# The convolution branch's output projection as seven products of quarters, with weight sums made by adding transfers

## The chip, the cores and the metric

The kernel runs on one core of a Trainium2 chip. The metric is the device time of one execution in microseconds (us). Three runs of the kernel before took 323.69, 324.17 and 324.25 us; their median is 324.17 us. The engines are named as in the profile: PE is TensorE's matrix multiplication and PEld its weight loads, DVE is VectorE, ACT is ScalarE, POOL is GpSimd, SP is SyncE. A q behind a name (SPq, POOLq) is the engine's sequencer, which issues transfers.

## The reference

One decoder layer on a sequence of 256 positions of width 1024, all in float32. What matters here, cut to its core:

```
h = rmsnorm(x, norm_g) * (1 + scale) + shift
q, k, v, g_attn, cb, cc, cx, g_conv, m_attn, m_conv = split(h @ w_in)
attn   = moba_attention(q, k, v, rel_bias)
y_attn = (attn * silu(g_attn)) @ w_o_attn
y_conv = (short_conv(cb, cc, cx, conv_w) * silu(g_conv)) @ w_o_conv
merged = sigmoid(m_attn) * y_attn + sigmoid(m_conv) * y_conv
out    = rmsnorm(x + gate * (merged @ w_out), final_g)
```

Every matrix here is 1024 wide, so `y_conv` is a product of a 256x1024 matrix with a 1024x1024 matrix. With both cut in four quarters, the rows of the left one at 128 and every other side at 512, it takes eight products of quarters and four additions in the usual way.

## The kernel before

Every float32 product is made of three passes. Each operand is split into a high part, rounded to the matrix unit's fast float32 format, and the rest, its low part; the product is high by high, high by low and low by high. For a weight tile (128x2048, 1 MB, one transfer on SP's queue, `load`, L58) ACT makes the high part and DVE the low part (`split`, L63: tiles named `...h` and `...l`). The raw tiles rotate through five buffers (L50), the high and the low parts through three each (L46), so a split waits until PE has finished with the tile three places back, and a load until the tile five places back is split.

The work that the change touches lies in the last third. `rows_half` (L362) computes two 128x512 results, one for each half t of the positions, from two weight tiles kh: `rows_mm` (L352) issues 12 matmuls for each t and tile, so a tile is 24 matmuls. In the order of the program: the merge gates `ma` and `mc` (L502 to L506, with ACT's sigmoid into SA and SC), then `merged(0)` and `merged(1)` (L537), each one column half n: `oa`, the attention branch's projection, then `oc`, the convolution branch's, from GA and GC, and the merging on DVE into MR (L541, L547, L548). `turned(n)` (L528) transposes MR on PE (tiles `pm`) and splits it into M, the left operand of the last projection `wo`, whose results are `ao`. `turned(0)` stands ahead of `oc` of the second half, `turned(1)` inside the first product `ao`.

A scheduler orders each engine's instructions by when it thinks that they can start, except those marked `pin`. Each engine runs its own list in order and waits on semaphores. PSUM's eight banks are handed out in turn (L52).

At the program's start `warm(WARM2)` (L254) puts matmuls on a tile of ones, whose results nobody reads, between the transposes of the first and of the second half of the normalised input (`px`, L205). ACT's first `hf` (L257) needs the transposes behind them, and PE's first real products need `hf`.

Of the kernel before, what the change touches and what calls it, by code (L numbers as in the profile page):

```python
# [39 lines left out]
def layer_kernel(ctx: ExitStack, tc, x, c, vec, wp_all, slab_all, onehot, final_g, out):  # L40
    nc = tc.nc
    x, out = x[0], out[0]

# [458 lines left out]
    for blk, dst in (("ma", SA), ("mc", SC)):  # L502
        for n in range(2):
            m = rows_half(blk, n, H)
            for t in range(2):
                nc.scalar.activation(dst[:, t, 512 * n:512 * (n + 1)], m[t], AF.Sigmoid)  # L506
# [30 lines left out]
    def merged(n):  # L537
        cols = slice(512 * n, 512 * (n + 1))
        ya = rows_half("oa", n, GA)
        for t in range(2):  # L540
            nc.vector.tensor_mul(MR[:, t, cols], ya[t], SA[:, t, cols])  # L541
        if n:
            turned(0)
        yc = rows_half("oc", n, GC)
        for t in range(2):
            p = tp.tile([P, 512], F32, tag="cx", name=f"yc{n}{t}", bufs=2)
            nc.vector.tensor_mul(p, yc[t], SC[:, t, cols])  # L547
            nc.vector.tensor_add(MR[:, t, cols], MR[:, t, cols], p)  # L548

    merged(0)  # L550
    merged(1)
# [145 lines left out]
```

## Time and profile before

| | |
|---|---|
| median of three runs | 324.17 us |
| the profiled execution | 324.17 us, of which 322.4 us are the span of the trace |
| outside the span | 1.77 us |
| PE busy | 312.5 us (97%) |
| DVE, ACT, POOL busy | 236.8, 176.2, 7.4 us |
| granted TensorE clock, mean | 0.994 of full speed |

The span runs from the first to the last instruction. Busy is not the same as bound: PE is the engine whose next instruction nearly always stands ready.

### The profile page before, as it was taken

The numbers are of one execution on the slowest core, as the hardware profiler recorded it, in microseconds if no ns is written. First come the engines' busy times: TensorE is split into PE (matmuls) and PEld (weight loads), VectorE is DVE, ScalarE is ACT, GpSimd is POOL, SyncE is SP. The second block draws the span as 40 slices with busy tenths as digits, with TensorE's granted clock in tenths as the row PEclk, the third lists the DMA queues.
The fourth block names the chain that finished last, engine by engine and source line by source line (L and its number), as shares of the span: only waits on it lengthen the run. The fifth ranks groups of instructions, "written<-read, shape, count | busy, mean of one in ns | idle before, by whom it ended". The sixth has DMA issues, their size and how long they took to land.

```text
span 322.4 us, 4585 instructions
## 1 busy us (share of the span) xinstructions
PE 312.5 (97%) x1794; PEld 275.3 (85%) x1794; DVE 236.8 (73%) x355; ACT 176.2 (55%) x271; POOL 7.4 (2%) x17
## 2 busy tenths in 40 slices
PE   7899999999999999999999999999999999999992
PEld 6799999888888988889888888888888888888892
DVE  3899994968599999786977787865243457657774
ACT  2655565863676777476666657474444433351430
POOL 2400000000000000000000000000000000000010
PEclk9999999999999999999999999999999999999997
DMA  7999999986676385836344577446465756300003
GB/s 271 413 411 409 407 415 416 399 330 259 246 266 236 138 355 184 287 126 256 130 138 188 197 254 269 138 151 233 159 232 164 285 162 239 132 0 0 0 2 130
DMA packets 14187, 72.74 MB, mean 226 GB/s; under 512 B 1510, under 2 KB 2902, under 8 KB 8022
## 3 DMA queue, kind: packets, MB, share of 16 engines
q1 hardware_dynamic: 12528, 70.40, 58.1%
q10 hardware_dynamic: 1606, 2.05, 1.8%
q8 instruction: 14, 0.23, 0.3%
q14 instruction: 7, 0.06, 0.0%
q0 software_dynamic: 32, 0.01, 0.0%
HBM read 71.39 MB, written 1.06 MB: 225 GB/s over the span
## 4 chain that ended last, share of the span: by engine, by line
PE 93%; DMA 2%; issue 1%; DVE 1%; ACT 1%; SPq 0%; POOL 0%; POOLq 0%; DVEq 0%; ACTq 0%
PE acc L198 15%; PE agc L340 5%; PE aga L340 5%; PE acc L340 5%; PE acx L340 5%; PE acb L340 5%; PE aga L342 2%; PE agc L342 2%; PE acb L342 2%; PE acx L342 2%; PE acc L342 2%; PE aoa L355 2%; PE ama L355 2%; PE av L355 2%; PE av L356 2%; PE aoc L356 2%
## 5 line engine op out<-in xcount | busy, mean ns | idle before, releaser
L381 DVE CUSTOM_DVE_ANT_0 gate<-gate,csb,vT 128x1024 f32<-128x1024 f32 x8 | 10.1, 1276 | 0.0
L161 DVE CUSTOM_DVE_ANT_0 ada<-ada,csb,msc 128x1024 f32<-128x1024 f32 x7 | 9.4, 1341 | 0.0
L161 DVE CUSTOM_DVE_ANT_0 ada<-ada,csb,vT 128x1024 f32<-128x1024 f32 x7 | 8.9, 1278 | 0.0
L589 POOL TENSOR_TENSOR rf<-ms,mhalf 128x1 f32<-128x1 f32 x2 | 1.7, 828 | 302.4 <-DVE ms L616 298.8
L326 ACT ACTIVATE lowcb<-acb 128x256 f32<-128x256 f32 x8 | 3.0, 371 | 6.1 <-PE acb L342 6.1
L347 ACT ACTIVATE M<-pm 128x512 fp32r<-128x512 f32 x4 | 2.2, 590 | 6.7 <-PE pm L534 6.7
L571 ACT ACTIVATE SQ<-TT 128x512 f32<-128x512 f32 x3 | 1.9, 628 | 7.1 <-DVE TT L566 7.1
L506 ACT ACTIVATE SC<-amc 128x512 f32<-128x512 f32 x4 | 2.4, 599 | 5.8 <-PE amc L357 5.8
L506 ACT ACTIVATE SA<-ama 128x512 f32<-128x512 f32 x4 | 2.4, 600 | 5.3 <-PE ama L357 5.3
L139 PE MATMUL wt<-ones 128*128 128x128 f32 x22 | 4.2, 362 | 1.0 <-DVE ones L127 1.0
L396 DVE TENSOR_TENSOR AX<-QK,AX 128x128 fp32r<-128x128 f32 (+1 forms) x16 | 5.1, 348 | 0.0
L70 DVE TENSOR_TENSOR oc00l<-woc,oc00h 128x2048 fp32r<-128x2048 f32 x1 | 2.3, 2292 | 3.8 <-ACT oc00h L69 3.8
L374 ACT ACTIVATE V<-av 128x512 f32<-128x512 f32 x4 | 2.4, 599 | 4.8 <-PE av L357 4.8
L70 DVE TENSOR_TENSOR oa00l<-woa,oa00h 128x2048 fp32r<-128x2048 f32 x1 | 2.3, 2291 | 3.6 <-ACT oa00h L69 3.6
L70 DVE TENSOR_TENSOR cb0l<-wcb,cb0h 128x2048 fp32r<-128x2048 f32 x1 | 2.3, 2293 | 3.6 <-ACT cb0h L69 3.6
L70 DVE TENSOR_TENSOR mc10l<-wmc,mc10h 128x2048 fp32r<-128x2048 f32 x1 | 2.3, 2291 | 3.6 <-ACT mc10h L69 3.6
L395 ACT ACTIVATE AX<-QK 128x128 fp32r<-128x128 f32 (+1 forms) x16 | 4.8, 364 | 0.0
L326 ACT ACTIVATE lowga<-aga 128x256 f32<-128x256 f32 x8 | 3.0, 373 | 3.3 <-PE aga L342 3.3
L139 PEld LDWEIGHTS wt<-ones 128*128 128x128 f32 x22 | 3.8, 267 | 1.0 <-DVE ones L127 1.0
L469 ACT ACTIVATE y<-cc,vT 128x256 f32<-128x256 f32 x8 | 3.9, 500 | 1.4 <-DVE cc L465 1.4
L326 ACT ACTIVATE lowgc<-agc 128x256 f32<-128x256 f32 x8 | 3.0, 373 | 3.0 <-PE agc L342 3.0
L70 DVE TENSOR_TENSOR oa11l<-woa,oa11h 128x2048 fp32r<-128x2048 f32 x1 | 2.3, 2293 | 3.1 <-ACT oa11h L69 3.1
(497 smaller groups left out, 1102.0 us busy)
## 6 DMA issues: line engine op xcount, KB each, us to landing
ada<-in_wp_dram SPq DMA_DIRECT2D x16, 512.0 KB, 10.2
slab<-in_slab_dram SPq DMA_DIRECT2D x16, 512.0 KB, 10.2
wv<-in_wp_dram SPq DMA_DIRECT2D x4, 1024.0 KB, 11.3
wcc<-in_wp_dram SPq DMA_DIRECT2D x4, 1024.0 KB, 5.6
wcx<-in_wp_dram SPq DMA_DIRECT2D x4, 1024.0 KB, 4.9
gate<-in_wp_dram SPq DMA_DIRECT2D x4, 1024.0 KB, 6.5
wcb<-in_wp_dram SPq DMA_DIRECT2D x4, 1024.0 KB, 5.4
wgc<-in_wp_dram SPq DMA_DIRECT2D x4, 1024.0 KB, 4.9
```

The costliest lines, as they stand in the source:

```text
L70: pin(nc.vector.tensor_sub(lo[:, s], raw[:, s], hi[:, s].bitcast(F32)))
L139: pin(nc.tensor.matmul(wt[:, 0:P], ones, ones, start=True, stop=True))
L161: pin(nc.vector.tensor_tensor_reduce(src, src, csb, vT[:, i:i + 1] if s else 1.0, bias(i, s), ALU.mult, ALU.add, scs[:, i, s:s + 1]))
L198: pin(nc.tensor.matmul(acc[j // 2][:, (j % 2) * S:(j % 2 + 1) * S], w[i][:, j * P:(j + 1) * P], x, start=(i == 0 and j // 2 not in opened) ...
L326: nc.scalar.activation(low, a[:, S:], AF.Copy)
L340: nc.tensor.matmul(a, hi[:, k, cols], rhs[:, k, :], start=(k == 0), stop=False)
L342: nc.tensor.matmul(a[:, S:], lo[:, k, cols], rhs[:, k, 0:S], start=False, stop=(k == KT - 1))
L355: nc.tensor.matmul(a, xh, hi[:, k4, cols], start=(first and k4 == 0), stop=False)
L356: nc.tensor.matmul(a, xh, lo[:, k4, cols], start=False, stop=False)
L381: nc.vector.tensor_tensor_reduce(src, src, csb, 1.0, vT[:, 24 + d:25 + d], ALU.mult, ALU.add, gcol[:, d:d + 1])
L395: nc.scalar.activation(hi, src, AF.Copy)
L396: nc.vector.tensor_sub(lo, src, hi.bitcast(F32))
```

## The change

`y_conv` is computed by Strassen's scheme in Winograd's form. With the four left quarters F(t, kh) and the four weight quarters, each of them one tile `oc` n kh, it takes seven products p1 to p7 instead of eight, each of 12 matmuls and one weight tile. Three of them (p1, p2, p3) use a weight quarter as it is, four use sums of two, three or four quarters:

- p7: oc10 + oc11, in the tile T2
- p5: oc10 + oc00, in the raw tile wt1
- p6: T2 + oc00, added onto the same tile once p7 has split it
- p4: T2 + oc01, added once p6 has split it

The sums are made by transfers on POOL's queue that add what they bring to what lies in the tile (`add_on`). The four left sums v1 to v4 are made on DVE from F, which is GC's high and low parts added together, and split into SX. Three PSUM banks hold the partial results for the whole stretch, and the ring of the others shrinks to five for it.

The products are woven between the tiles of `mc` and `oa`; on PE the order is now ma, p7, mc00, p5, mc01, p1, mc10, p6, mc11, p2, oa00, p4, oa01, p3, oa10, `turned(0)`, oa11, and then `ao`. The transposition of the gate column (`pgt`), from which gb is read back, moves behind p4. The merging on DVE is now in SA (`joined`). T2, and after it gb and fg, take the place of csb, cs, gb and fg in one 8 KB tile. The x tile XR is loaded later. And WARM2 falls from 5 to 3. The diff's core:

```diff
-WARM2 = 5
+WARM2 = 3
...
+    ring, turn = list(range(8)), [0]
+
+    def bank(name, at=None):
+        if at is None:
+            at = ring[turn[0] % len(ring)]
+            turn[0] += 1
+        return ps.tile([P, 512], F32, tag=f"b{at}", name=name)
...
+    F = raw_tile([P, 2048], "F").rearrange("p (k n) -> p k n", k=KT)
+    nc.vector.tensor_add(F, GC[:, :, 0:S].bitcast(F32), GC[:, :, S:].bitcast(F32))
...
+    def both(v, dst):
+        nc.scalar.activation(dst[:, :, 0:P], v, AF.Copy)
+        nc.vector.tensor_sub(dst[:, :, P:], v, dst[:, :, 0:P].bitcast(F32))
...
+    T2 = big.tile([P, 2048], F32, tag="W2", name="T2")
+    def add_on(t, key):
+        nc.gpsimd.dma_start(t, wp_all[UNIT[key]], accum_op=ALU.add)
+
+    nc.sync.dma_start(T2, wp_all[UNIT["oc", 1, 0]])
+    add_on(T2, ("oc", 1, 1))
+    first = load(("oc", 1, 0), "wt1")
+    add_on(first, ("oc", 0, 0))
+    ring[:] = range(3, 8)
+    turn[0] = 0
+    bA, bB, bC = [bank(f"str{i}", i) for i in range(3)]
+
+    def product(a, raw, name, first, s=0, t=0, kh=0):
+        hi, lo = split(raw.rearrange("p (k n) -> p k n", k=4), [P, 4, 512], name)
...
+    product(bB, T2, "p7", True, s=3)
+    q7 = kept(bB, "cx", "q7")
+    add_on(T2, ("oc", 0, 0))
+    a = pair("mc", 0)
+    rows_tile("mc", 0, 0, H, a)
+    product(bC, first, "p5", True, s=1)
+    rows_tile("mc", 0, 1, H, a)
...
+    product(bB, T2, "p6", False, s=2)
+    u3 = tp.tile([P, 512], F32, tag="cc", name="u3", bufs=2)
+    nc.vector.tensor_add(u3, bB, q1)
+    nc.vector.tensor_sub(q7, u3, q7)
+    nc.vector.tensor_sub(u3, bC, u3)
+    rows_tile("mc", 1, 1, H, a)
...
+    product(bA, w21, "p2", False, t=0, kh=1)
+    add_on(T2, ("oc", 0, 1))
+    nc.vector.tensor_mul(part(0, 0), part(0, 0), bA)
+    a = pair("oa", 0)
+    rows_tile("oa", 0, 0, GA, a)
+    product(bB, T2, "p4", False, t=1, kh=1)
...
+    joined(0, a)
+    product(bC, load(("oc", 1, 1), "woc22"), "p3", False, s=4)
...
+    turned(0)
+    rows_tile("oa", 1, 1, GA, a)
+    joined(1, a)
+    ring[:] = range(8)
```

Three places show how the lists of the engines move. On ACT, where the high parts of the weight tiles are made in the stretch of the gates, the list before has one tile `...h` after another:

```order
L69 ACTIVATE mc00h<-wmc_2317 128x2048 [waits DMAHW0_49,Activation_49]
L69 ACTIVATE mc01h<-wmc_2347 128x2048 [waits DMAHW1_49,PE_49,Activation_49]
L506 ACTIVATE SA<-ama_2251 128x512 [waits PE_49]
L506 ACTIVATE SA<-ama_2252 128x512 [waits PE_49]
L69 ACTIVATE mc10h<-wmc_2381 128x2048 [waits DMAHW2_49,DVE_49]
L69 ACTIVATE mc11h<-wmc_2411 128x2048 [waits DMAHW3_49,DVE_49,PE_49]
```

The same engine now, from the second half of the gate mc to p4 (DMAHW are transfers of SP's and ACT's queues, DMASW those of POOL's):

```order
L514 ACTIVATE SC<-amc_2359 128x512 [waits PE_49]
L74 ACTIVATE p6h<-T_2330 128x2048 [waits DMASW3_49,DVE_49]
L579 ACTIVATE q_2456<-str_2336 128x512 [waits PE_49]
L74 ACTIVATE mc11h<-wmc_2510 128x2048 [waits DMAHW4_49,DVE_49]
L74 ACTIVATE p2h<-woc_2543 128x2048 [waits DMAHW5_49,DVE_49,PE_49]
L74 ACTIVATE oa00h<-woa_2565 128x2048 [waits DMAHW6_49,DVE_49,PE_49]
L514 ACTIVATE SC<-amc_2458 128x512 [waits PE_49]
L514 ACTIVATE SC<-amc_2459 128x512 [waits PE_49]
L74 ACTIVATE p4h<-T_2330 128x2048 [waits DMASW4_49,DVE_49]
L74 ACTIVATE oa01h<-woa_2621 128x2048 [waits DMAHW0_49,DVE_49,PE_49]
```

The product tiles stand between the tiles of the gates and of `oa`, and p6h and p4h wait for a transfer of POOL's queue; what follows them in ACT's list stands behind that wait.

On POOL the list of the changed kernel, from the start's last work to the end, is this (before, nothing stood between `rvd` and `rf`):

```order
L278 DMA rvd<-rv 8x384 [waits Activation_49]
L555 DMA T_2330<-in_wp_dram 128x2048 [waits DMAHW4_49,DVE_49,PE_49]
L555 DMA wt_2333<-in_wp_dram 128x2048 [waits DMAHW3_49,DMAHW5_49,DMAHW2_49,DMAHW6_49,DMAHW0_49,DMAHW7_49,DVE_49,Activation_49]
L555 DMA T_2330<-in_wp_dram 128x2048 [waits DMASW1_49,DVE_49]
L555 DMA T_2330<-in_wp_dram 128x2048 [waits DMASW3_49,DVE_49]
L703 TENSOR_TENSOR rf_2892<-ms_2890,mhalf 128x1 [waits DVE_49,Pool_49]
```

The third and the fourth adding transfer each wait for the one before on the same tile and for DVE's low part of the product that used the tile's older contents.

On DVE, ahead of the last projection, the list before ran so (`M<-pm` is the low part of the transposed merged rows, `yc` and `MR` the merging of the second half):

```order
L541 TENSOR_TENSOR MR<-aoa_2586,SA 128x512
L70 TENSOR_TENSOR o00l<-wo_2731,o00h 128x2048
L348 TENSOR_TENSOR M<-pm_2649,M 128x2x256
L348 TENSOR_TENSOR M<-pm_2656,M 128x2x256
L70 TENSOR_TENSOR o01l<-wo_2737,o01h 128x2048
L547 TENSOR_TENSOR yc_2725<-aoc_2663,SC 128x512
```

and now so:

```order
L75 TENSOR_TENSOR o00l<-wo_2756,o00h 128x2048
L636 TENSOR_TENSOR SC<-SC,q_2355 128x512
L647 TENSOR_TENSOR wo_2809<-wo_2809,gf 128x4x256
L75 TENSOR_TENSOR o01l<-wo_2762,o01h 128x2048
L353 TENSOR_TENSOR M<-pm_2708,M 128x2x256
L353 TENSOR_TENSOR M<-pm_2715,M 128x2x256
L629 TENSOR_TENSOR SA<-SA,aoa_2675 128x512
L631 TENSOR_TENSOR SA<-SA,SC 128x512
```

The low parts of M come behind both splits of `wo`'s first tiles, and the merging of the second half follows them at once.

## Rows read from the trace of the kernel before

**Rows 1.** The page: span, busy time of the first engines, chain that ended last.
```profile
span 322.4 us, 4585 instructions
PE 312.5 (97%) x1794; PEld 275.3 (85%) x1794; DVE 236.8 (73%) x355; ACT 176.2 (55%) x271; POOL 7.4 (2%) x17
...
PE 93%; DMA 2%; issue 1%; DVE 1%; ACT 1%; SPq 0%; POOL 0%; POOLq 0%; DVEq 0%; ACTq 0%
```

**Rows 2.** Waits of PE, whole span: engine, tile, releaser: us, times, longest.
```profile
PE px L205 <- DVE xx L243: 2.0, 1, 2.0
PE wt L139 <- DVE ones L127: 1.0, 1, 1.0
PE acc L198 <- ACT hf L257: 0.7, 1, 0.7
```

**Rows 3.** Timeline, PE, 281 to 293: start us, us, engine, line, operation, tiles.
```profile
281.31 1.03 PE L534 MATMUL pm<-ident,MR 128*128 128x128 f32 x8
...
282.64 0.39 PE L357 MATMUL aoc<-oc10h,GC 128*128 128x512 f32 x1
...
293.07 0.39 PE L355 MATMUL ao<-o00h,M 128*128 128x512 f32 x1
```

**Rows 4.** Timeline, ACT and DVE, one weight tile's split.
```profile
270.62 1.92 ACT L69 ACTIVATE oc10h<-woc 128x2048 fp32r<-128x2048 f32 x1 [3.52 <-PE aoc L357]
...
272.57 2.29 DVE L70 TENSOR_TENSOR oc10l<-woc,oc10h 128x2048 fp32r<-128x2048 f32 x1 [0.50 <-ACT oc10h L69]
```

**Rows 5.** Windows: stretch, length, busy PE, PEld, DVE, ACT, POOL, clock, DMA, GB/s.
```profile
205.00:227.00 22.00, 22.00 (x100) 18.20 (x99) 13.40 (x12) 11.12 (x13) 0.00 (x0) 1.00 0.53 187
227.00:249.00 22.00, 22.00 (x99) 18.16 (x98) 9.17 (x4) 10.08 (x9) 0.00 (x0) 1.00 0.56 194
249.00:271.00 22.00, 22.00 (x99) 18.18 (x98) 12.01 (x9) 8.39 (x7) 0.00 (x0) 1.00 0.59 214
271.00:293.00 22.00, 22.00 (x103) 18.31 (x102) 14.63 (x13) 8.26 (x6) 0.00 (x0) 1.00 0.24 92
```

**Rows 6.** A group of DVE instructions on 128x512: count | busy us, mean ns | idle.
```profile
L548 DVE TENSOR_TENSOR MR<-MR,yc 128x512 f32<-128x512 f32 x4 | 2.8, 692 | 0.1
```

**Rows 7.** DMA issues, whole span: count, KB each, median us to landing.
```profile
woc<-in_wp_dram SPq DMA_DIRECT2D x4, 1024.0 KB, 4.9
...
BI<-rvd ACTq DMA_DIRECT2D x1, 1024.0 KB, 18.5
...
rvd<-rv POOLq DMA_DIRECT2D x1, 12.0 KB, 5.3
```

**Rows 8.** Timeline, DVE, ACT, POOL, 281 to 297, around the last projection.
```profile
281.50 1.92 ACT L69 ACTIVATE o00h<-wo 128x2048 fp32r<-128x2048 f32 x1 [3.53 <-PE aoa L357]
283.32 1.07 ACT L347 ACTIVATE M<-pm 128x512 fp32r<-128x512 f32 x2
...
285.66 1.28 DVE L348 TENSOR_TENSOR M<-pm,M 128x512 fp32r<-128x512 f32 x2
```

**Rows 9.** Timeline, all engines, 7 to 13, the start.
```profile
9.83 1.28 PE L139 MATMUL wt<-ones 128*128 128x128 f32 x10
...
9.94 0.51 ACT L240 ACTIVATE xx<-xx,r 128x256 f32<-128x256 f32 x1 [0.95 <-POOL r L145]
10.01 2.22 POOL L241 TENSOR_SCALAR xx<-xx,r 128x768 f32<-128x768 f32 x1
10.66 0.08 DVE L154 DVE_READ_ACCUMULATOR2_ANT scs<- 128x1 f32 x1
...
10.95 0.38 PE L205 MATMUL px<-ident,xx 128*128 128x128 f32 x2
11.37 0.56 ACT L257 ACTIVATE hf<-px,scs 128x256 f32<-128x256 f32 x1 [0.92 <-DVE csb L220]
...
12.95 0.82 PE L205 MATMUL px<-ident,xx 128*128 128x128 f32 x6
```

**Rows 10.** Timeline, PE, first matmuls of the span.
```profile
1.05 2.93 PE L139 MATMUL wt<-ones 128*128 128x128 f32 x12 [1.05 <-DVE ones L127]
```

More of the change, by code (lines that the diff above doesn't have):

```diff
@@ L50, in layer_kernel @@
     RAW_BUFS = 5
-    def bank(name):
-        return ps.tile([P, 512], F32, tag="acc", name=name, bufs=8)
+    ring, turn = list(range(8)), [0]
[4 more added lines that the diff above has]
+        return ps.tile([P, 512], F32, tag=f"b{at}", name=name)
     def raw_tile(shape, name):
@@ L79, in layer_kernel @@
     xnT = big.tile([P, KT, S], F32, tag="BI", name="xnT")
-    csb = big.tile([P, D], F32, tag="AG", name="csb")
-    cs = big.tile([P, P], F32, tag="GB", name="cs")
+    wide = big.tile([P, 2 * D], F32, tag="W2", name="wide")
+    csb, cs = wide[:, 0:D], wide[:, D:D + P]
     crows = const.tile([KT, P], F32, name="crows")
@@ L497, in layer_kernel, with rows_tile @@
         gated("ga", AT, GA, j)
-    gb = big.tile([P, D], F32, tag="GB", name="gb")
-    XR = big.tile([P, 2, D], F32, tag="YB", name="XR")
     SA = big.tile([P, 2, D], F32, tag="V", name="SA")
     SC = big.tile([P, 2, D], F32, tag="BI", name="SC")
[L502 to L506, printed above, removed]
+    def rows_tile(blk, n, kh, xs, a):
+        raw = load((blk, n, kh), f"w{blk}{n}{kh}").rearrange("p (k n) -> p k n", k=4)
+        hi, lo = split(raw, [P, 4, 512], f"{blk}{n}{kh}")
+        for t in range(2):
+            rows_mm(a[t], xs, t, hi, lo, 4 * kh, slice(0, 512), kh == 0, kh == 1)
@@ new lines, in gate_rows, with pair @@
+    def gate_rows(blk, n, dst, a):
+        for t in range(2):
+            nc.scalar.activation(dst[:, t, 512 * n:512 * (n + 1)], a[t], AF.Sigmoid)
+    def pair(blk, n):
+        return [bank(f"a{blk}{n}{t}") for t in range(2)]
+    for n in range(2):
+        a = pair("ma", n)
+        for kh in range(2):
+            rows_tile("ma", n, kh, H, a)
+        gate_rows("ma", n, SA, a)
+    F = raw_tile([P, 2048], "F").rearrange("p (k n) -> p k n", k=KT)
+    nc.vector.tensor_add(F, GC[:, :, 0:S].bitcast(F32), GC[:, :, S:].bitcast(F32))
@@ new lines, in layer_kernel, with quarter, quad @@
+    SX = [big.tile([P, 2, 4, S], F32R, tag=tag, name=f"SX{tag}") for tag in ("YB", "AT")]
+    SX = {1: SX[0][:, 0], 3: SX[0][:, 1], 2: SX[1][:, 0], 4: SX[1][:, 1]}
+    def quarter(t, kh):
+        return F[:, 4 * kh:4 * kh + 4, t * P:(t + 1) * P]
+    def quad(tag, name):
+        return tp.tile([P, 4, P], F32, tag=tag, name=name, bufs=2)
+    def both(v, dst):
+        nc.scalar.activation(dst[:, :, 0:P], v, AF.Copy)
+        nc.vector.tensor_sub(dst[:, :, P:], v, dst[:, :, 0:P].bitcast(F32))
@@ new lines, in layer_kernel @@
+    v3 = quad("cc", "v3")
+    nc.vector.tensor_sub(v3, quarter(0, 0), quarter(1, 0))
+    both(v3, SX[3])
+    v1 = quad("cx", "v1")
+    nc.vector.tensor_sub(v1, quarter(1, 0), quarter(1, 1))
+    both(v1, SX[1])
+    v2 = quad("y", "v2")
+    nc.vector.tensor_sub(v2, v1, quarter(0, 0))
+    both(v2, SX[2])
+    v4 = quad("cc", "v4")
+    nc.vector.tensor_add(v4, v2, quarter(0, 1))
+    both(v4, SX[4])
+    T2 = big.tile([P, 2048], F32, tag="W2", name="T2")
+    def add_on(t, key):
+        nc.gpsimd.dma_start(t, wp_all[UNIT[key]], accum_op=ALU.add)
@@ new lines, in layer_kernel @@
+    nc.sync.dma_start(T2, wp_all[UNIT["oc", 1, 0]])
[7 more added lines that the diff above has]
+        hi, lo = split(raw.rearrange("p (k n) -> p k n", k=4), [P, 4, 512], name)
+        for k in range(4):
+            if s:
+                xh, xl = SX[s][:, k, 0:P], SX[s][:, k, P:]
+            else:
+                xh = GC[:, 4 * kh + k, t * P:(t + 1) * P]
+                xl = GC[:, 4 * kh + k, S + t * P:S + (t + 1) * P]
+            for w, xp, end in ((hi, xh, False), (lo, xh, False), (hi, xl, k == 3)):
+                nc.tensor.matmul(a, xp, w[:, k], start=(first and k == 0 and w is hi and xp is xh), stop=end,
+                                 skip_group_check=True)
@@ new lines, in kept, with part @@
+    def kept(a, tag, name):
+        t = tp.tile([P, 512], F32, tag=tag, name=name, bufs=2)
+        nc.scalar.activation(t, a, AF.Copy)
+        return t
+    def part(t, n):
+        return SC[:, t, 512 * n:512 * (n + 1)]
+    product(bB, T2, "p7", True, s=3)
[5 more added lines that the diff above has]
+    rows_tile("mc", 0, 1, H, a)
+    gate_rows("mc", 0, SC, a)
+    w11 = load(("oc", 0, 0), "woc11")
@@ new lines, in layer_kernel @@
+    product(bA, w11, "p1", True, t=0, kh=0)
+    q1 = kept(bA, "y", "q1")
+    a = pair("mc", 1)
+    rows_tile("mc", 1, 0, H, a)
+    product(bB, T2, "p6", False, s=2)
[4 more added lines that the diff above has]
+    rows_tile("mc", 1, 1, H, a)
+    gate_rows("mc", 1, SC, a)
+    nc.vector.tensor_mul(part(1, 1), part(1, 1), u3)
+    w21 = load(("oc", 0, 1), "woc21")
@@ L507, in layer_kernel @@
+    product(bA, w21, "p2", False, t=0, kh=1)
[4 more added lines that the diff above has]
+    product(bB, T2, "p4", False, t=1, kh=1)
+    nc.vector.tensor_add(q1, bB, q1)
+    nc.vector.tensor_mul(part(1, 0), part(1, 0), q1)
+    gf = big.tile([P, 2 * D], F32, tag="W2", name="gf")
+    gb, fg = gf[:, 0:D], gf[:, D:]
     pgt = bank("pgt")
@@ L513, in layer_kernel, with joined @@
     nc.scalar.dma_start(gb, bass.AP(tensor=gd.tensor, offset=gd.offset, ap=[[0, P], [1, D]]))
-    nc.sync.dma_start(XR, x.rearrange("(t p) d -> p t d", p=P))
+    rows_tile("oa", 0, 1, GA, a)
+    def joined(n, a):
+        cols = slice(512 * n, 512 * (n + 1))
+        for t in range(2):
+            nc.vector.tensor_mul(SA[:, t, cols], SA[:, t, cols], a[t])
+        for t in range(2):
+            nc.vector.tensor_add(SA[:, t, cols], SA[:, t, cols], SC[:, t, cols])
+    joined(0, a)
+    product(bC, load(("oc", 1, 1), "woc22"), "p3", False, s=4)
+    nc.vector.tensor_sub(q7, bC, q7)
+    nc.vector.tensor_mul(part(0, 1), part(0, 1), q7)
+    a = pair("oa", 1)
+    rows_tile("oa", 1, 0, GA, a)
     M = big.tile([P, KT, 512], F32R, tag="H", name="M")
@@ L524, in wo_split @@
         wo[n, kh] = split(raw, [P, 4, 512], f"o{n}{kh}", 1, pin)
-    MR = big.tile([P, 2, D], F32, tag="AT", name="MR")
+    MR = SA
     def turned(n):
@@ L535, in turned @@
             put(pm.rearrange("p (a b) -> p a b", a=2), M, j)
[L537 to L551, printed above, removed]
+    turned(0)
+    rows_tile("oa", 1, 1, GA, a)
+    joined(1, a)
+    ring[:] = range(8)
     for kh in range(2):
         wo_split(0, kh)
+    XR = big.tile([P, 2, D], F32, tag="YB", name="XR")
+    nc.sync.dma_start(XR, x.rearrange("(t p) d -> p t d", p=P))
     TT = big.tile([P, 2, D], F32, tag="AT", name="TT")
-    SQ = big.tile([P, 2, 512], F32, tag="V", name="SQ")
-    fg = big.tile([P, D], F32, tag="AG", name="fg")
+    SQ = big.tile([P, 2, 512], F32, tag="BI", name="SQ")
     nc.sync.dma_start(fg, bass.AP(tensor=final_g.tensor, offset=final_g.offset, ap=[[0, P], [1, D]]))
```

## The prediction

> **What bounds the kernel now.** The page comes first: PE is busy for 97% of the span and makes up 93% of the chain that ended last [rows 1]. A busy PE may still be waiting inside its queue, so the waits of PE come second: it waits three times in the whole span, 3.7 us in all, and each time in the start [rows 2]. From there on PE goes from one matmul to the next. Third, the timeline of the stretch that the change replaces: between the third matmul of the tile oc10 and the first of `ao` lie 46 matmuls and 293.07 - 282.64 = 10.43 us [rows 3], so one of 512 columns takes 0.2267 us, without a gap at the tiles' borders. Fourth, the windows from the gates to the last projection: in these 88 us PE is busy throughout, DVE for 49.2 us, ACT for 37.9 us, and the transfers take 0.24 to 0.59 of the DMA engines [rows 5]. So a matmul removed there is time gained, if whatever feeds PE keeps up.
>
> The sum is made against the profiled execution, 324.17 us, which is its span of 322.4 us and 1.77 us around it. It is also the median of the runs shown.
>
> **What goes.** `oc` was four tiles of 24 matmuls, 96; it becomes seven products of 12, 84. Twelve times 0.2267 us is 2.72 us. PE's list gains nothing: `pgt` and the transposes stay, and the products of sums are matmuls of the same shape.
>
> **What comes, beside PE.** DVE gets three more low parts of weight tiles, 2.29 us each [rows 4], F (as many elements, 2.3 us), four sums and four low parts of sums and five more merging steps, 13 times 0.69 us [rows 6]: 18 us. ACT gets three more high parts of 1.92 us [rows 4] and six copies of 128x512 at about 0.6 us, by the pair of such high parts in 1.07 us [rows 8]: 9 us. The idle time of these windows, 38.8 and 50.1 us, holds both [rows 5]. So the totals cost nothing; the places have to be looked at.
>
> *The splits.* A split starts when PE is done with the tile three places back. Before, two tiles of 5.44 us lay between; now one of 5.44 and one of 2.72 us, 8.16 us. A split starts 0.2 us behind its tile (o00h at 281.50, the tile's end where `pm` begins at 281.31 [rows 3, 8]) and ends 272.57 + 2.29 - 270.62 = 4.24 us later [rows 4]. Spare: 3.7 us. Cost nothing.
>
> *The adding transfers.* For the times that follow I count back from `ao` at 293.07 - 2.72 = 290.35 in PE's new order: oa11 begins at 284.91, the transposes at 284.03 (they cost 0.88 us up to the next matmul, 281.31 to 282.64 less two matmuls [rows 3]), oa10 at 278.6, p3 at 275.9, p4 at 267.6, p6 at 251.3, p1 at 243.1, p5 at 234.9, p7 at 226.8. The last of the four transfers is the tight one. It starts when T2's split for p6 is done: p6h can begin when mc01 is through at 243.1, behind 0.2 us and a sigmoid of 0.6 us in ACT's list, so the split ends at 248.1. p4's split must start at 267.6 + 0.2 - 4.24 = 263.6, since its low part is first read by the second matmul. The transfer has 15.5 us from issue to landing. Behind p4h in ACT's list stand oa01h and p3h, but their tiles are needed only 2.7 us and more after p4. The third, from T2's split for p7 at about 220.9 (ma01 ends 10.9 us ahead of p7) to 247.3, has 26 us. The second adds to wt1, whose load is issued once ma00 is split, by 205 at the latest: 20 us and more. The first lies far ahead.
>
> No adding transfer is in the trace. A plain 1 MB load lands after 4.9 us; the slowest 1 MB transfer, BI, after 18.5 us; the one transfer of POOL's queue takes 5.3 us for 12 KB, so the queue itself can't be costlier than that [rows 7]. From below 4.9 us, from above 18.5 us: a stall of 0 or of 18.5 - 15.5 = 3.0 us. The nearest row is the weight load, which brings the same bytes from the same place; as the tile has to be read as well, I take twice, 9.8 us, and no stall. A gain below nothing is excluded, as PE waits for no weights now.
>
> The Trainium skill (Collectives: The Full Stack, "The bandwidth ceiling: the fold count and why AG ≠ RS ≠ AR") says that an addition in the DMA engines costs no time of its own but needs two source reads, and gives 62.28 against 32.35 GB/s for copy and reduction. By it the transfer is at most 9.8 us and nothing stalls, as by the choice above; by the BI row 3 us are lost. No run here shows it yet. It is a reason against the second rival below, no proof, since it was measured between cores.
>
> *Other transfers.* SP's queue carries 1 MB more of plain loads in this stretch. XR waits for p5 and fg for p4's split, both over 20 us ahead of their first use behind `ao`; what stands behind them on the queue waits for later splits anyway. Nothing.
>
> *The join.* turned(0) now has one tile, not two, between it and `ao`. o01h starts when oa10 is through, 284.2, and ends at 286.15; M's high parts follow by 287.1, as in [rows 8]; o01l ends at 288.4, and the pair of M's low parts (1.28 us [rows 8]) at 289.65. `ao` needs them at once, since its bank is freed by the second of them: 0.7 us spare. Ahead of o01l stands the product of `wo` with gb, which needs two small transfers behind `grow` (about 272.5); at 5.3 us each, as the one on POOL's queue [rows 7], gb is there by 283.1, and DVE comes to it at 284.0. Then the four merging steps of the second half, 4 x 0.69, end at 292.4; turned(1) wants them at 290.35 + 2.72 = 293.07, 0.7 us spare again. I count nothing, with little to spare.
>
> **The start.** Two warm-up products fewer are 4 of 10 instructions that began 1.12 us ahead of `px` (9.83 to 10.95): 0.45 us [rows 9]. The profile puts hf's wait down to DVE, but hf reads px and scs alone, and scs is written at 10.74; px ends at 11.33 and hf starts at 11.37. So PE is what it waits for. px can move to 10.50, as its operand is ready at 10.45. The next transposes, at 12.95, can move as well: POOL's part is done at 12.23. From there on PE is dense, so the gain lasts. Bounds: 0 (another wait takes its place) and 0.45; I take 0.45.
>
> Sum: 324.17 - 2.72 - 0.45 = 321.0 us.
>
> **Rivals.** *The fourth adding transfer is late.* POOL's transfer reads, adds and writes in turn and takes four times the plain load, 19.6 us. p4 then stalls for 4.1 us: 325.1 us, slower. It decides from 15.5 us on, eats the gain at 18.7 us, and beyond 26 us p6 stalls too. For it: nothing in the trace shows such a transfer cheap, three of them form one chain through T2, and p4h holds up ACT's list. Against: the window is three times the plain load. At BI's 18.5 us the time would be 324.0, no change.
>
> *The join is late.* One split of 2.29 us more ahead of M's low parts, because DVE's list gives it precedence or a transfer lands late, eats the 0.7 us and costs 1.6: 322.6 us. For it: the smallest reserve on the path, twice. Against: its inputs are done earlier by the sums above.
>
> *The clock at the start.* The first 12 matmul instructions on ones took 2.93 us, 0.244 each [rows 10]; the later ten 0.112 [rows 9]. If with less warm-up PE fell back to that rate for as long, half of 2.9 us is lost: 322.5 us. Against: PE's wait ahead of the real products gets no longer, and the recorded clock of the later windows is 1.00 [rows 5]. The Trainium skill (TensorE: Matmul & The Clock Gate, "Part 1: The HAM clock gate") says that activity is what releases the clock, 2.4 instead of 1.2 GHz; by that rule the change takes away some of it, and the time is this rival's. The trace agrees as far as the first matmuls are half as fast.
>
> That the change doesn't remove the work is no rival: the matmuls are counted in PE's list.
>
> **Chances.** Forecast 321.0 us: 0.63, with a range of its own from 320.4 to 321.7, the low end for instruction handling that nobody counted, the upper end for no gain at the start. Join late 0.12, clock 0.04, transfer a little late (15.5 to 19 us: 321 to 324.5) 0.08, transfer far too late 0.13. Within 0.2%, 323.5 to 324.8, is what a measurement can't tell from no change. Faster: 0.63 + 0.12 + 0.04 and 0.03 of the little late, 0.82; same 0.05; slower 0.13. The range from 320.3 to 323.5 holds all but about 0.2.
>
> **What would show it.** Right: 12 matmuls fewer, PE's waits still those of the start alone, `px` at about 10.5, the adding transfers landing in about 10 us, `ao` some 3.2 us earlier than at 293.07. Wrong: p4 or p6 waiting for p4h or p6h, which wait for a transfer of POOL's queue; `ao` or `pm` waiting for DVE's M or SA; `hf` released by something else at about 11.4; or 0.24 us per instruction again behind the warm-up.

## The result and the profile after

The changed kernel takes 321.06 us (median of 4 executions, 320.79 to 321.27) against 324.13 us: a ratio of 0.9907, 95% interval 0.989 to 0.9925. The forecast was 321.0 us. It gains 0.75% to 1.1%.

The page after, with the rows that answer to [rows 1]:

```profile
span 319.0 us, 4604 instructions
PE 310.4 (97%) x1778; PEld 273.7 (86%) x1778; DVE 253.1 (79%) x372; ACT 184.6 (58%) x280; POOL 11.8 (4%) x21
...
PE 95%; issue 1%; DVE 1%; ACT 1%; POOL 0%; POOLq 0%; DVEq 0%; ACTq 0%
```

PE is still the bound. Its list is 16 instructions shorter: the twelve matmuls and four of the warm-up. DVE is busy for 16.3 us more and ACT for 8.4, near the 18 and 9 counted. PE's waits, which answer to [rows 2], are again those of the start alone:

```profile
PE wt L144 <- DVE ones L132: 1.0, 1, 1.0
PE px L210 <- DVE xx L248: 0.7, 1, 0.7
PE acc L203 <- ACT hf L262: 0.7, 1, 0.7
```

PE's timeline, the first matmuls of five tiles, and `ao` as in [rows 3]:

```profile
226.04 0.39 PE L574 MATMUL str<-p7h,SXYB 128*128 128x512 f32 x1
...
250.53 0.39 PE L574 MATMUL str<-p6h,SXAT 128*128 128x512 f32 x1
...
266.85 0.39 PE L574 MATMUL str<-p4h,GC 128*128 128x512 f32 x1
...
283.32 1.03 PE L658 MATMUL pm<-ident,SA 128*128 128x128 f32 x8
284.11 0.48 PE L360 MATMUL aoa<-oa11h,GA 128*128 128x512 f32 x1
...
289.65 0.39 PE L360 MATMUL ao<-o00h,M 128*128 128x512 f32 x1
```

`ao` is 3.42 us earlier than at 293.07, and the span is 3.4 us shorter (322.4 to 319.0). Every place that the prediction had counted back from 290.35 (226.8, 251.3, 267.6, 284.03, 284.91) came 0.7 to 0.8 us earlier, in the right distance from each other: 0.7 is what the earlier arrival of x (0.30) and the shorter warm-up (0.39) gave together, as the rows of the start below show.

The windows of the same four stretches as [rows 5] (the last one is shorter here), with the DMA share in the last column but one:

```profile
205.00:227.00 22.00, 22.00 (x99) 18.21 (x98) 17.16 (x18) 12.49 (x17) 0.87 (x1) 1.00 0.97 274
227.00:249.00 22.00, 22.00 (x99) 18.22 (x98) 12.74 (x6) 13.29 (x10) 0.87 (x1) 1.00 0.80 296
249.00:271.00 22.00, 22.00 (x99) 18.15 (x98) 15.19 (x11) 11.92 (x8) 0.00 (x0) 1.00 0.84 263
271.00:290.00 19.00, 19.00 (x89) 15.80 (x89) 17.44 (x18) 7.44 (x7) 0.00 (x0) 1.00 0.39 139
```

The added work lies in idle time, as forecast. The DMA share rose more than the bytes: 0.53 to 0.97 in the first stretch (1.8 times), at 187 to 274 GB/s (1.5 times).

**The start** needs one more row of before: both kernels wait for the same transfer, the second half of x, and that comes at another time in each execution. The ACT timeline of before, the first work on it:

```profile
7.84 1.06 ACT L238 ACTIVATE xx<-xx 128x1024 f32<-128x1024 f32 x1 [3.33 <-DMA xx<-in_x_dram]
```

and after, all engines, to be read against [rows 9]:

```profile
7.54 1.06 ACT L243 ACTIVATE xx<-xx 128x1024 f32<-128x1024 f32 x1 [3.03 <-DMA xx<-in_x_dram]
...
9.54 0.83 PE L144 MATMUL wt<-ones 128*128 128x128 f32 x6
...
10.21 0.43 PE L210 MATMUL px<-ident,xx 128*128 128x128 f32 x2
...
10.68 0.56 ACT L262 ACTIVATE hf<-px,scs 128x256 f32<-128x256 f32 x1 [0.53 <-PE px L210]
...
11.29 1.13 PE L203 MATMUL acc<-hf,slab 128*128 128x256 f32 x4 [0.66 <-ACT hf L262]
```

The last row is PE's first real product, `acc`. In before it is this:

```profile
11.98 1.13 PE L198 MATMUL acc<-hf,slab 128*128 128x256 f32 x4 [0.65 <-ACT hf L257]
```

x came 0.30 us earlier in this execution; that is no gain of the change. Counted from x, hf starts after 10.68 - 7.54 = 3.14 us instead of 11.37 - 7.84 = 3.53. So the shorter warm-up gave 0.39 us, and the profile now names PE's `px` as what releases hf. The whole span counted from x is 319.0 - 7.54 = 311.46 against 322.4 - 7.84 = 314.56 us: 3.10 us. The start has 0.39 of them, which leaves 2.71 for the twelve matmuls. This measure (span less x's arrival) is used for the experiments too; it is good to about 0.1 us, as the spans are printed to that. A second one needs neither x nor the span: from `acc` to `ao` pass 293.07 - 11.98 = 281.09 us in before and 289.65 - 11.29 = 278.36 in after, 2.73 us less.

### The profile page after: what moved, and what is told of

It is laid out like the page before. It is cut to its first block, busy times and chain, and to the rows that moved or that the text cites. A ratio compares the mean times of both kernels' runs of the same rounds, so it can differ in the third digit from the quotient of the medians.

```text
span 319.0 us, 4604 instructions
## 1 busy us (share of the span) xinstructions
PE 310.4 (97%) x1778; PEld 273.7 (86%) x1778; DVE 253.1 (79%) x372; ACT 184.6 (58%) x280; POOL 11.8 (4%) x21
## 4 chain that ended last, share of the span: by engine, by line
PE 95%; issue 1%; DVE 1%; ACT 1%; POOL 0%; POOLq 0%; DVEq 0%; ACTq 0%
PE acc L203 15%; PE str L574 6%; PE agc L345 5%; PE aga L345 5%; PE acc L345 5%; PE acx L345 5%; PE acb L345 5%; PE aga L347 2%; PE acx L347 2%; PE acb L347 2%; PE agc L347 2%; PE acc L347 2%; PE aoa L362 2%; PE aoa L360 2%; PE ama L360 2%; PE av L360 2%
## 5 line engine op out<-in xcount | busy, mean ns | idle before, releaser
L386 DVE CUSTOM_DVE_ANT_0 gate<-gate,wide,vT 128x1024 f32<-128x1024 f32 x8 | 10.1, 1278 | 0.0
L166 DVE CUSTOM_DVE_ANT_0 ada<-ada,wide,msc 128x1024 f32<-128x1024 f32 x7 | 9.4, 1342 | 0.0
L166 DVE CUSTOM_DVE_ANT_0 ada<-ada,wide,vT 128x1024 f32<-128x1024 f32 x7 | 8.9, 1277 | 0.0
L555 POOL DMA_DIRECT2D T<-in_wp_dram x3 | 2.7, 884 | 162.1 <-DMA T<-in_wp_dram 120.2
L75 DVE TENSOR_TENSOR p6l<-T,p6h 128x2048 fp32r<-128x2048 f32 x1 | 2.3, 2293 | 3.6 <-ACT p6h L74 3.6
L75 DVE TENSOR_TENSOR p5l<-wt,p5h 128x2048 fp32r<-128x2048 f32 x1 | 2.3, 2294 | 3.6 <-ACT p5h L74 3.6
L74 ACT ACTIVATE oa11h<-woa 128x2048 fp32r<-128x2048 f32 x1 | 1.9, 1917 | 4.9 <-DVE SA L631 4.9
L203 PE MATMUL acc<-hf,slab 128*128 128x256 f32 x16 | 3.9, 386 | 0.7 <-ACT hf L262 0.7
L331 ACT ACTIVATE lowcx<-acx 128x256 f32<-128x256 f32 x8 | 3.0, 377 | 2.4 <-PE acx L347 2.3
```

The source lines that it names most:

```text
L166: pin(nc.vector.tensor_tensor_reduce(src, src, csb, vT[:, i:i + 1] if s else 1.0, bias(i, s), ALU.mult, ALU.add, scs[:, i, s:s + 1]))
L203: pin(nc.tensor.matmul(acc[j // 2][:, (j % 2) * S:(j % 2 + 1) * S], w[i][:, j * P:(j + 1) * P], x, start=(i == 0 and j // 2 not in opened) ...
L331: nc.scalar.activation(low, a[:, S:], AF.Copy)
L386: nc.vector.tensor_tensor_reduce(src, src, csb, 1.0, vT[:, 24 + d:25 + d], ALU.mult, ALU.add, gcol[:, d:d + 1])
```

## The experiments

"From x" is the span less the arrival of x, in the profiled execution, good to about 0.1 us; the ratio is to the kernel before on the same chip.

| run | median us (executions) | ratio, 95% | from x |
|---|---|---|---|
| before | 324.13 (4) | | 314.56 |
| after | 321.06 (4) | 0.9907, 0.989 to 0.9925 | 311.46 |
| again (after once more) | 320.69 (4) | 0.9906, 0.989 to 0.9923 | 311.50 |
| before_warm3 | 323.61 (11) | 0.999, 0.9981 to 0.9998 | 314.17 |
| warm5 | 321.65 (5) | 0.992, 0.9907 to 0.9934 | 311.84 |
| warm2 | 320.90 (4) | 0.9909, 0.9894 to 0.9924 | 311.41 |
| warm1 | 322.47 (12) | 0.9955, 0.993 to 0.998 | 313.18 |
| warm0 | 322.76 (12) | 0.9955, 0.9932 to 0.9978 | 312.97 |
| plain | 320.85 (5) | 0.9907, 0.9891 to 0.9922 | 311.50 |
| wide | 321.82 (5) | 0.9932, 0.9919 to 0.9944 | 311.90 |
| quarter | 326.63 (4) | 1.0073, 1.0057 to 1.0089 | 316.70 |
| rows32 | 325.97 (10) | 1.0024, 0.9991 to 1.0058 | 313.40 |
| twice | 330.54 (4) | 1.0197, 1.0184 to 1.0211 | 320.34 |
| alone | 323.19 (1) | | 313.69 |

### The two gains apart: warm5 and before_warm3

```
-WARM2 = 3
+WARM2 = 5
```

in the changed kernel (warm5), and the other way round in the kernel before (before_warm3).

> The changed kernel with five warm-up products ahead of px again instead of three; nothing else differs. Theory (PE's own list holds px, and hf waits for px): four instructions of 0.112 us more ahead of px, so px and hf come 0.45 us later than with three, nothing behind them takes it back, and the time is 321.06 + 0.45 = 321.5 us. Rival (hf came earlier in the changed kernel only because x arrived 0.3 us earlier in that execution, and the warm-up is hidden): 321.06 us, no change.

> The kernel before with three warm-up products instead of five, and none of the other changes. Theory (the start and the seven products are two separate gains that add up): 324.13 - 0.45 = 323.7 us, and the seven products are then worth 323.7 - 321.06 = 2.6 to 2.7 us, twelve matmuls of 0.2267. Rival (the start gives nothing): 324.1 us, and the seven products with what stands around them give all 3.1 us, more than twelve matmuls cost.

The medians stand where the theory put them within their spread (321.65 for 321.5, 323.61 for 323.7). From x the sum closes within the 0.1 us of that measure: warm5 lies 0.38 us above after, before_warm3 0.39 below before, and between kernels with the same warm-up are 314.56 - 311.84 = 2.72 and 314.17 - 311.46 = 2.71 us. From `acc` to `ao` it closes more finely: 292.35 - 11.28 = 281.07 us in before_warm3 (281.09 in before) and 289.88 - 11.50 = 278.38 in warm5 (278.36 in after), so 2.71 us for either warm-up. The seven products are worth twelve matmuls (2.72 counted) and nothing else that these rows show, and the two gains add up. ACT in warm5, the rows that were 3.14 us apart in after:

```profile
7.36 1.06 ACT L243 ACTIVATE xx<-xx 128x1024 f32<-128x1024 f32 x1 [2.85 <-DMA xx<-in_x_dram]
...
10.88 0.56 ACT L262 ACTIVATE hf<-px,scs 128x256 f32<-128x256 f32 x1 [0.92 <-DVE wide L225]
```

They are 3.52 us apart, as in before, and the releaser is again a DVE copy that hf doesn't read.

### The clock: warm2, warm1, warm0, again

```
-WARM2 = 3
+WARM2 = 2
```

and likewise 1 and 0; again has 3.

> The changed kernel with no warm-up product at all between the first transposes and px. Theory: with three, px already starts when its operand xx is there (PE waits 0.7 us for it), so PE's list has nothing more to give: 321.0 us, between 320.9 and 321.1, with the granted clock of 9 to 13 us still 1.00. Rival (activity ahead of px is what keeps the clock up): the granted clock of this stretch falls, the matmuls of px and acc take up to twice as long for a while, and the time goes up by 0.5 to 1.5 us, to 321.6 to 322.5.

> The changed kernel with one warm-up product ahead of px instead of three. With none, px came no earlier after x than with three (3.15 against 3.14 us up to hf), and the granted clock fell to 0.52 in 11 to 13 us. Theory (from three downwards only the clock is at stake, and three is not far from where it falls): px no earlier than 2.67 us after x is there, the granted clock under 1.00 in 11 to 15 us in some executions, 321.1 to 322.8 us with a spread of over 1 us. Rival (one product is enough to keep the clock up): 321.0 us with a spread of 0.5 us, clock 1.00.

> The changed kernel with two warm-up products ahead of px instead of three. Theory (two is already too few in some executions, as one and none are): some executions at 321.0 and some at 322 to 325 us, a spread of over 1.5 us. Rival (two still keep the clock up): 321.0 us, all within 0.7 us. In both px comes no earlier than 2.67 us after x is there, so nothing is gained over three.

> The changed kernel once more, unchanged, for its spread on this chip beside the other runs. Theory (three warm-up products keep the clock up in every execution): 321.06 us, all executions within 0.7 us, granted clock 1.00 from 9 to 20 us. Rival (three is at the edge and it falls in some executions, as with one and none): single executions of 322 us and more.

In all of them hf starts 3.13 to 3.16 us behind x: less warm-up than three gains nothing more. With two the time is that of three (320.61 to 321.53, against 320.59 to 321.41 in again, four executions each). With one or none it runs from 320.9 to 324.9 us from execution to execution. Windows of warm0, the granted clock in the last column but two:

```profile
9.00:11.00 2.00, 1.24 (x10) 0.76 (x8) 1.96 (x5) 0.73 (x2) 1.81 (x3) 1.00 1.03 418
11.00:13.00 2.00, 1.61 (x4) 1.34 (x5) 1.15 (x3) 1.97 (x5) 1.39 (x2) 0.52 1.03 414
13.00:15.00 2.00, 2.00 (x11) 1.75 (x10) 1.07 (x2) 0.90 (x3) 0.39 (x1) 0.63 1.03 412
```

PE runs at its lower level, 1.2 GHz, from 11 us to about 14.5, and from x the span is 1.5 us longer than with three (312.97 to 311.46). That is the price of the prediction's clock rival (1.5 us). Ahead of the fall PE had waited 1.9 and 0.5 us for `px`'s operands, where after has one wait of 0.7; but plain, with three warm-up products, waited 1.5 and 1.0 us there and kept its clock. So warm0's theory fell to its rival (whose 321.6 to 322.5 us the median passes by 0.3), warm1's held (single executions go beyond its range), and warm2's fell: with two warm-up products nothing is lost in four executions. The slowest executions with one or none, 324.6 to 324.9 us, lie 3.5 to 3.9 us above after's median, more than the 1.5 us of the one in these windows; no trace shows them, so what they lost is open. The Trainium skill (TensorE: Matmul & The Clock Gate, "Part 1: The HAM clock gate") says that the throttled clock is the default and that activity releases it; by that rule less warm-up can cost, and the 0.52 of these windows agrees.

### The adding transfers hidden or not: plain

```
-nc.gpsimd.dma_start(t, wp_all[UNIT[key]], accum_op=ALU.add)
+nc.gpsimd.dma_start(t, wp_all[UNIT[key]])
```

> The changed kernel with the four adding transfers turned into plain transfers of the same bytes on the same queue at the same places; the sums of weight quarters are left out, so four of the seven products have a wrong operand. Theory (the adding transfers are hidden, the last one with some 5 us to spare): the time stays at 321.06 within 0.2 us, while the landing falls from 9.4 to 10.1 us to 5 or 6, and the share of the DMA engines in 205 to 227 us falls from 0.97 to about 0.6. Rival (the added reading slows the loads of weights beside it and by that PE): faster by 0.3 us or more.

No gain: from x 311.50 against 311.46 us. The landings fell to 5.0 to 6.7 us, about as expected; the share of the DMA engines did not fall to 0.6:

```profile
205.00:227.00 22.00, 22.00 (x100) 18.24 (x99) 18.02 (x20) 12.60 (x15) 0.92 (x2) 1.00 0.76 287
```

So of the rise from 0.53 in before to 0.97 in after, about half comes from the bytes (0.76 at 287 GB/s) and half from the adding. Transfers of after (count, KB each, median us to landing), and the queue's packets (count, MB, share of 16 engines' span):

```profile
q0 software_dynamic: 608, 4.21, 7.1%
...
wmc<-in_wp_dram SPq DMA_DIRECT2D x4, 1024.0 KB, 7.0
...
T<-in_wp_dram POOLq DMA_DIRECT2D x3, 1024.0 KB, 9.5
```

and of plain:

```profile
q0 software_dynamic: 608, 4.21, 3.5%
...
wmc<-in_wp_dram SPq DMA_DIRECT2D x4, 1024.0 KB, 4.8
...
T<-in_wp_dram POOLq DMA_DIRECT2D x3, 1024.0 KB, 5.1
```

The same packets take twice the engine time when they add, and the loads of `mc` beside them land 2.2 us later. PE sees none of it. The Trainium skill (Collectives: The Full Stack, "The bandwidth ceiling: the fold count and why AG ≠ RS ≠ AR") puts the cost of an addition at the second source read, about twice a copy; 7.1% against 3.5% agrees with that factor, here between HBM and SBUF.

### The window of the fourth transfer: twice, quarter, rows32

Each of the three runs has one of the added lines:

```
     add_on(T2, ("oc", 0, 1))
+    add_on(T2, ("oc", 1, 1))                                                   # twice
+    nc.gpsimd.dma_start(T2[:, 0:512],  wp_all[UNIT["oc", 1, 1]][:, 0:512],  accum_op=ALU.add)  # quarter
+    nc.gpsimd.dma_start(T2[0:32, :],   wp_all[UNIT["oc", 1, 1]][0:32, :],   accum_op=ALU.add)  # rows32
```

> The changed kernel with a fifth adding transfer of 1 MB chained behind the fourth on the same tile T2, so that p4 gets a wrong sum of three quarters. Theory (the fourth transfer has a window of 15 to 15.5 us from its issue, and one takes 9.4 to 10.1): the first lands at 257.0, the second follows at once and lands at 266.4 to 267.5, p4's split ends 4.24 us after that, at 270.6 to 271.7, where p4's second matmul stood at 267.08: PE waits 3.6 to 4.7 us in p4, on p4h or p4l, and the time is 324.7 to 325.8 us. Rival (two transfers of one queue overlap, or p4 has more slack than counted): PE waits for nothing, 321.1 us.

> The changed kernel with a fifth adding transfer of a quarter of the size (256 KB) chained behind the fourth on T2, so that p4 gets a wrong operand in a quarter of its columns. Theory (window of 15 to 15.5 us): it lands 2.5 to 4 us behind the fourth, at 259.5 to 261, some 12 to 13.5 us after the fourth was issued; p4's split starts up to 1.5 us later than at 259.38 and ends before 265.5, ahead of p4's second matmul at 267.08. PE waits for nothing, 321.1 us, within 0.3. Rival (the split for oa01, which stands behind p4h in ACT's list, or the merging behind p4l on DVE, has less slack than p4): a wait of 0.5 to 1.5 us on oa01h, oa01l or p3h, 321.6 to 322.6 us.

> The run with the fifth adding transfer of 256 KB once more, but as 32 rows of 8 KB instead of 128 rows of 2 KB, so that p4 gets a wrong operand in 32 of its 128 rows. In the first form it landed 8.6 us after its issue, though its packets took a quarter of the engines' time of a full one, beside a load of wo that landed after 8.3 us. Theory (the queues of one DMA engine take turns packet by packet, so eight packets an engine last as long as the eight of wo beside them, whatever their size): two packets an engine, the transfer lands 3 to 4.5 us after its issue, at 261.2 to 262.7, p4's split ends by 267.0, PE waits 0 to 0.5 us in p4, and the time is 321.1 to 321.6 us. Rival (an adding transfer chained behind another costs 8 us or more whatever its size): landing after 8 to 9 us, PE waits 3 us in p4, the granted clock falls behind it, 326 to 327 us.

Waits of PE in twice, quarter and rows32, those in p4:

```profile
PE str L574 <- ACT p4h L74: 4.9, 1, 4.9
PE str L574 <- DVE p4l L75: 1.5, 1, 1.5
```

```profile
PE str L574 <- DVE p4l L75: 1.8, 1, 1.8
...
PE str L574 <- ACT p4h L74: 1.3, 1, 1.3
```

```profile
PE str L574 <- DVE p4l L75: 1.7, 1, 1.7
```

The wait is where the prediction's first rival put it, but none of the three times was as expected: the fifth transfers were slower than counted, the small ones most of all, and a wait cost more than its length. The fifth one of quarter, on POOL and then ACT:

```profile
248.14 0.87 POOL L555 DMA_DIRECT2D T<-in_wp_dram  x1 [26.33 <-DVE p6l L75]
258.21 0.87 POOL L609 DMA_DIRECT2D T<-in_wp_dram  x1 [9.20 <-DMA T<-in_wp_dram]
...
266.93 1.91 ACT L74 ACTIVATE p4h<-T 128x2048 fp32r<-128x2048 f32 x1 [6.89 <-DMA T<-in_wp_dram]
```

It took 8.6 us for 256 KB, and 7.4 in rows32; twice's took 12.0 for 1 MB. With the landing as measured, the predicted window of 15.5 us from the fourth transfer's issue holds in all three within 0.4 us. Landing less issue is 264.9 - 248.0 = 16.9 us in rows32, 266.8 - 248.1 = 18.7 in quarter and 270.7 - 248.4 = 22.3 in twice: 1.4, 3.2 and 6.8 us beyond 15.5, and PE waits 1.7, 3.1 and 6.4.

The price of a wait was wrong. Counted from x, 3.1 us of waiting cost 5.2 and 6.4 us cost 8.9. Windows of twice behind its wait:

```profile
271.00:272.00 1.00, 0.00 (x0) 0.00 (x0) 0.00 (x0) 1.00 (x1) 0.00 (x0) 0.90 0.00 0
272.00:273.00 1.00, 0.30 (x1) 0.29 (x1) 0.32 (x1) 1.00 (x2) 0.00 (x0) 0.50 0.00 0
...
278.00:279.00 1.00, 1.00 (x4) 0.75 (x4) 1.00 (x1) 0.00 (x0) 0.00 (x0) 0.68 0.39 78
```

PE finds its clock at 1.2 GHz after the wait and keeps it to 278.6 us. In quarter the clock is down from 271.3 to 274.7: 3.4 us at half speed lose 1.7 us by estimate, which is most of the 2.1 us that the wait cost beyond its length. In rows32, whose wait was 1.7 us, the profiled execution kept its clock and lost 1.9 us; of ten executions four took 322.8 to 323.5 us at a mean clock of 0.996 to 0.998, five 325.9 to 326.7 at 0.991 to 0.993 and one 327.7 at 0.988. The lower mean clock goes with the longer time, but of the longer executions there is no trace: whether they also waited longer is not shown.

### A small adding transfer by itself: alone

```
+    Z = big.tile([P, 2048], F32, tag="GA", name="Z")
+    for rows, cols, op in ((P, 2048, ALU.bypass), (P, 512, ALU.bypass), (P, 512, ALU.add),
+                           (32, 2048, ALU.add), (P, 2048, ALU.add)):
+        nc.gpsimd.dma_start(Z[0:rows, 0:cols], wp_all[UNIT["oc", 0, 0]][0:rows, 0:cols], accum_op=op)
```

> The changed kernel with five more transfers on POOL's queue into a tile Z that nothing reads, each chained behind the one before, from the end of oa11 (about 289.7 us) on, where the DMA engines have nothing else to do: plain 1 MB, plain 256 KB, adding 256 KB (128 rows of 2 KB), adding 256 KB (32 rows of 8 KB), adding 1 MB. Its end may be late, since POOL's last work stands behind them; only the landing times are read. In the two runs with a fifth transfer of 256 KB it landed after 8.6 and 7.4 us, beside loads of 1 MB. Theory (an adding transfer's own time follows its bytes, and the loads beside it made those slow): the packets of 1 MB took 94 us of engine time, 5.9 us on 16 engines, so alone it lands after 7 to 8 us and 256 KB after 3 to 4 us, plain 256 KB after 2 to 3 us. Rival (a fixed cost of each adding transfer): 7 us or more for 256 KB too, in both forms, beside 2 to 3 us for the plain one.

POOL's timeline; each issue waits for the transfer before it. (The end comes 2.2 us later from x than in after, as foreseen.)

```profile
290.56 0.56 POOL L667 DMA_DIRECT2D Z<-in_wp_dram  x1 [41.95 <-PE aoa L362]
296.06 0.57 POOL L667 DMA_DIRECT2D Z<-in_wp_dram  x1 [4.94 <-DMA Z<-in_wp_dram]
299.70 0.91 POOL L667 DMA_DIRECT2D Z<-in_wp_dram  x1 [3.08 <-DMA Z<-in_wp_dram]
304.24 0.82 POOL L667 DMA_DIRECT2D Z<-in_wp_dram  x1 [3.63 <-DMA Z<-in_wp_dram]
309.19 0.90 POOL L667 DMA_DIRECT2D Z<-in_wp_dram  x1 [4.13 <-DMA Z<-in_wp_dram]
```

From one issue to the next pass 3.6 us for plain 256 KB, 4.5 and 5.0 for the two adding ones. From issue to landing the plain one took 3.4 us, the adding ones 4.0 and 4.7, a little above the ranges expected. There is no fixed cost of 7 us. (The last one, 1 MB, took 9.3 us, but it ran beside the stores of the output, so it says nothing.) That the loads beside them made the 8.6 and 7.4 us is what the traces of the DMA queues bear out. In quarter POOL's queue moved no packet from the issue at 258.21 to 262.3 us, while SP's queue took 0.91 of the engines' time, and its packets then ran to 266.4 among SP's; alone, the first came within 1.9 us of its issue at 299.70 and the last before 303.6. In rows32 the first came 2.8 to 3.1 us after the issue, alone 1.5 to 1.8. How one engine chooses between its queues is not settled. My theory of turns row by row gave 3 to 4.5 us for rows32, and it took 7.4. The Trainium skill (DMA: Bandwidth & Descriptors, "Queues, rings and completion order") says that an engine drains a whole packet of one queue, typically 9 to 17 descriptors, before it turns to the next; by that a short transfer would wait for the long ones beside it whatever its form. Both forms were slow (8.6 and 7.4 us), which agrees, but no row here follows the turns of a single engine.

### The join's reserve: wide

```
-            g = gb[:, D - S:]
+            c0 = 0 if kh else S
+            g = gb[:, D - 512 + c0:]
...
-            pin(nc.vector.tensor_mul(raw[:, :, S:], raw[:, :, S:], g))
+            pin(nc.vector.tensor_mul(raw[:, :, c0:], raw[:, :, c0:], g))
```

> The changed kernel with one of the two products of the last projection's weights with gb, the one ahead of o01l in DVE's list, over 512 columns instead of 256, so that a quarter of the output's columns gets its gain once too often in half of the sum; the order on all engines is unchanged. Theory (M's low parts are 0.7 us ahead of ao): the product takes 2.3 us instead of 1.22, M's low parts end at 290.0 instead of 288.96, and ao, at 289.65, waits 0.4 us for M; the merging of the second half still ends ahead of its transposes. 321.06 + 0.4 = 321.5 us. Rival (more slack than counted, or DVE makes it up): no wait of PE behind the start, 321.1 us. Second rival (the merging has less slack and turned(1) waits too): 0.8 to 1.1 us more, 321.9 to 322.2 us.

The timeline of DVE and PE in wide, around the first matmul of `ao`:

```profile
288.49 1.28 DVE L353 TENSOR_TENSOR M<-pm,M 128x512 fp32r<-128x512 f32 x2
...
289.82 0.50 PE L360 MATMUL ao<-o00h,M 128*128 128x512 f32 x1 [0.16 <-DVE M L353]
```

The theory holds: the product is 1.07 us longer, M's low parts end 0.95 us later counted from x (289.77 - 7.40 against 288.96 - 7.54), `ao` waits for M and starts 0.31 us later from x (289.82 - 7.40 against 289.65 - 7.54), and the span is 0.44 us longer (0.4 was expected); what the last 0.1 us are, in a measure good to 0.1, isn't shown. The reserve was the 0.7 us that the prediction worked out from rows of before.

## Why the prediction was right, point by point

**What goes.** 2.72 us predicted; 2.71 from `acc` to `ao`, and 2.71 and 2.72 from x, between kernels with equal warm-up.

**The start.** 0.45 predicted, 0.39 measured. PE's `px` did move by 0.44 us (from x: 3.11 to 2.67), but its two transposes took 0.43 instead of 0.38. That hf waited for PE, against what the profile named, was right: hf moved with the warm-up in both kernels. That the sum, 321.0, stands 0.06 us from the median is in part luck: the start gave 0.06 us less than counted, the median of before was 324.13 and not 324.17, and x's arrival, which no term holds, moves single executions by more than that.

**The splits.** Spare 3.7 us, and no wait. Those of p4 in after:

```profile
259.38 1.91 ACT L74 ACTIVATE p4h<-T 128x2048 fp32r<-128x2048 f32 x1
...
261.32 2.29 DVE L75 TENSOR_TENSOR p4l<-T,p4h 128x2048 fp32r<-128x2048 f32 x1 [1.11 <-ACT p4h L74]
```

p4h waits for nothing but its place in ACT's list; p4l is through at 263.6, 3.5 us ahead of p4's second matmul (267.08).

**The adding transfers.** 9.8 us chosen, 9.4 to 11.8 measured (median 10.1); the fourth was issued at 247.59, half a microsecond ahead of the count (PE's places were 0.7 ahead), and took 9.4. Plain showed that they are hidden, and three runs that the window is 15.5 us within 0.4. The reason given, that the tile has to be read as well, fits the doubled engine time. (The sentence on the Collectives page calls what it argues against the second rival; meant was the first.)

**The join.** Predicted: M's low parts 0.7 us ahead of `ao`. The rows that answer to [rows 8], DVE and ACT in after:

```profile
276.28 0.35 ACTq L623 DMA_DIRECT2D gf<-gd  x1
276.76 1.92 ACT L74 ACTIVATE oa11h<-woa 128x2048 fp32r<-128x2048 f32 x1 [4.93 <-DVE SA L631]
...
287.68 1.28 DVE L353 TENSOR_TENSOR M<-pm,M 128x512 fp32r<-128x512 f32 x2
```

and ACT in twice, where DVE's SA came later:

```profile
285.70 1.92 ACT L74 ACTIVATE oa11h<-woa 128x2048 fp32r<-128x2048 f32 x1 [4.10 <-DMA gd<-grow]
```

M's low parts end at 288.96, `ao` starts at 289.65: 0.69 us. What the prediction missed stands above it. The issue of gb's read-back waits in ACT's list until `gd` has landed, and oa11h stands behind it: 4.93 us of idle ACT. (In after the profile puts this wait down to DVE's SA, in twice to the transfer; in both oa11h starts 0.48 us behind the start of that issue, at 276.28 and 285.22.) It cost nothing, since oa11's low part was through at 281.0 and PE came to it at 284.11, but this queue had not been looked at.

**The rivals.** None came. Their points were right where they could be tried (15.5 us; 0.7 us), but a late transfer was priced too low: 4.1 us of stall would not have made 325.1 us. A wait of 3.1 us cost 5.2, and most of the 2.1 us on top is the clock that fell behind it. At the 18.7 us that were given as break-even, quarter was 2.3 us slower than the kernel before on its chip (324.31). The clock rival did not come with three warm-up products; with none it came, at its price.

## What to carry to other kernels

On a kernel whose PE never waits behind its start, a matmul less is worth its pitch (here 2.71 us for twelve, 2.72 counted), and what replaces it must be looked at place by place: here the reserves were 15.5 - 9.4 = 6.1 us for the last transfer and 0.7 for the join. Price a stall of PE with a lower clock behind it as well, not with its length alone: of the three stalls in p4, two were followed by one. Before reading a difference of 0.3 us, subtract the arrival of the first input, which moved by a whole microsecond between executions.

## What the runs showed of the hardware

- In after an adding transfer of 1 MB from HBM into SBUF lands after 9.4 to 11.8 us, in plain one without the addition on the same queue after 5.0 to 6.7; the packets take twice the engine time (7.1% against 3.5%), and the issue holds POOL for 0.87 us instead of 0.54.
- 256 KB added took 4.0 us alone and 8.6 beside loads of 1 MB as 128 rows of 2 KB, 4.7 and 7.4 as 32 rows of 8 KB.
- A PE that waited 3.1 us in the middle of the kernel (quarter) ran at 1.2 GHz from 271.3 to 274.7 us, one that waited 6.4 us (twice) until 278.6.
- The second half of x came between 7.36 and 8.40 us, and the whole span moved with it (plain: 8.40 and 319.9 us, after: 7.54 and 319.0).
